# A second Strassen level for P2 beside P3 in the SwiGLU groups, with sums in dead tiles and an earlier state update in retention

## The chip, the cores and the metric

The kernel runs on one core of a Trainium2 chip. The metric is the device time of one execution in microseconds (us): before the change 2171.48 us is the median of three runs (2169.85 to 2172.43). The core has a matrix engine (TensorE, PE in the profile; PEld is its weight load), a vector engine (VectorE, DVE), a scalar engine (ScalarE, ACT), GpSimd (POOL), and SyncE (SP), which here issues the DMAs. Each engine takes its own instructions in the order in which the program lists them and waits on semaphores for what the others must deliver.

## The reference

One layer of a streaming encoder on x of 1024 tokens by 1024 channels, all in float32: a SwiGLU with weight 0.5, a mixing sub-layer, a second SwiGLU, a final norm.

```python
def swiglu_ffn(x, w_in, w_out):                      # D_FF = 2816
    gate, up = jnp.split(x @ w_in, 2, axis=-1)
    return (jax.nn.silu(gate) * up) @ w_out

h = h + 0.5 * swiglu_ffn(rmsnorm(h, norm_ffn1), ffn1_w_in, ffn1_w_out)
u = rmsnorm(h, norm_mix)
proj = u @ w_in                                      # q, k, v, g, p, two gates
ret = retention(q, k, v)                             # 4 heads, chunks of 64, decaying state
ret = head_norm(ret) * jax.nn.silu(g_ret)
pool_out = multiscale_pool(p, pool_w, pool_scale)    # windows 2, 4, 8, 16
merged = gate0 * (ret @ w_ret_up) + gate1 * (pool_out @ w_pool_up)
h = h + merged @ w_out
h = h + 0.5 * swiglu_ffn(rmsnorm(h, norm_ffn2), ffn2_w_in, ffn2_w_out)
return rmsnorm(h, norm_final)
```

In retention a state is carried over the tokens: `new_state = state * decay + k^T v`, and each chunk of tokens adds the product of its queries with the state before it.

## The kernel before

**Precision.** Every operand of a matmul is held as two tiles, a high half (a cast by ScalarE, line 151) and a low half (the source less that cast, by VectorE, line 152); `split` makes both. `mm3` (lines 171 to 173) issues three matmuls for one product: high by high, high by low, low by high. One product of a group is four `mm3`, that is 12 matmuls of 128x512.

**Strassen's scheme.** A group is a block of the weights, 1024 channels by two blocks of 128 columns, against all 1024 tokens. `strassen` computes it in Winograd's form with seven products in place of eight. The group's two weight blocks are loaded as raw tiles `ra` (L11, L12) and `rb` (L21, L22); the activations stand ready as R11, T2, T1, T3, R21, R22 and T4 (class `Next`). The group is a list of seven steps, each with a part that prepares weights and a part with the products: 0 P1 = L11 R11, 1 P6 = S2 T2, 2 P5 = S1 T1, 3 P7 = S3 T3, 4 P2 = L12 R21, 5 P3 = S4 R22, 6 P4 = L22 T4. Their sums form in PSUM banks a, b and e:

```python
S1 = L21 + L22;  S2 = S1 - L11;  S3 = L11 - L21;  S4 = L12 - S2
a = P1 + P2;  b = P1 + P6 (+ P5) + P3;  e = P7 + P4
BY_OPERAND = (0, 4, 1, 3, 2, 6, 5);  BY_SUM = (0, 3, 1, 4, 2, 6, 5)
```

**Pairs and the second level.** `pairs` (line 548) runs groups two by two. The first groups go step by step side by side (BY_OPERAND); from the group `start` on, P3 of both groups of a pair is left out of the single groups and done together by `third` (line 491): as both have the same operand R22, the two S4 stand side by side as one 2x2 block matrix, and seven products of quarter size (42 matmuls of 128x256) take the place of twice 12 of 128x512. The second level wants sums of the weights (`s12`, `s34`, lines 495 to 507, 128x256 pieces on VectorE) and differences of the blocks of R22, called y1 to y4. These four tiles are made once per operand by `Next.blocks` (line 329).

**The SwiGLUs.** In the first, the names begin with a: `ffn_in` "a" runs a plain group 0 and then groups 11, 1, 12, 2, 13, ... (21 of them), with start=4; in the second, they begin with c: 22 groups 0, 11, 1, 12, ..., start=2. A group's results are scaled by the norm's root (`rms`, line 639), gate goes through silu, and gate by up is the hidden block. When groups k and k + 11 are both there, the four differences that the down projection (`ffn_out`, "b" and "d") wants are made (lines 660 to 670) and stored to memory: t, b, r and m.

**What sets the order.** `Flow.run` takes the steps one by one: it calls the preparing part of a step four steps (LOOK) ahead of its products, and after each step's products up to two entries of a queue `flow.back`, in which scaling, silu, gating, the y blocks and the norm's work are put by `flow.add`. `flow.until` drains that queue until something named is ready. Evacuations of a bank are put in with high priority (`soon`), which sets them ahead in their engine's order. Tiles come from pools of a fixed number: 5 of weights, 4 raw, 9 of `t4` and 4 of `tl` (a thousand columns each), 8 of `c2` (512 columns), 6 + 2 PSUM banks. All loads and stores go out on SP's queue in program order.

**Retention.** For each of 4 heads there are two halves of the tokens (`Unit`, nh 0 and 1). `products` (line 1381) computes the first state (`update(0)`), the inner products, the part across chunks from that state (`across`, bank xb), and for nh 0 then the second state (`update(1)`). `update` (line 1357) runs 12 matmuls of 128x256 into a bank, copies or adds it to `now`, and splits that into high and low halves named `state`.

The functions that the change touches:

Of the kernel before, what the change touches and what calls it, by code (L numbers as in the profile page):

```python
# [89 lines left out]
def block_kernel(ctx: ExitStack, tc, x, x_tok, vecs, f1_in, f1_out, w_in, w_v, pool_w, w_ret, w_pool, w_o,  # L90
# [160 lines left out]
    class Next(Norm):  # L251


        def __init__(self, name, gain, keep=None):
            super().__init__(name)
            self.gain, self.keep = gain, keep
            self.M, self.Y, self.made, self.tiles, self.t1s, self.rb = {}, {}, {}, {}, {}, None

# [69 lines left out]

        def blocks(self):


            def differences(z):
                x = []
                for i in range(2):
                    m = self.M["R22", 2 * i + z]
                    x.append(c2(f"{self.name}x{i}{z}"))
                    tt(x[i], m[:, 0].bitcast(F32), m[:, 1].bitcast(F32), ADD)
                (x00, x01), (x10, x11) = ([half_of(v, j) for j in range(2)] for v in x)
                for n, p, q in (("y1", x01, x00), ("y3", x11, x01), ("y2", x11, None), ("y4", x10, None)):
                    if n not in self.made:  # L340

                        self.made[n] = sb.tile([P, 2, H], F32R, tag="tl", bufs=N_TL, name=f"{self.name}{n}")

                    to = {"y1": x00, "y3": x01, "y2": x00, "y4": x00}[n]
                    tt(to, p, x00 if q is None else q, SUB)
                    m, at = self.made[n], (LO, HI)[z]
                    split(m[:, 0, at], m[:, 1, at], to)
                if z:
                    self.Y.update(self.made)

            return [lambda z=z: differences(z) for z in range(2)]

        def block(self, n, z):

            if n in self.Y or isinstance(n, str):
                flow.until(lambda: n in self.Y)
                return parts(self.Y[n], (LO, HI)[z])
            return parts(self.operand("R22", 2 * n[0] + z), (LO, HI)[n[1]])

# [30 lines left out]

    def strassen(nx, wa, wb, name, evac, end, begin=None, shared=False):

# [14 lines left out]
        def prep_w(n):  # L407
            def go():
                if n == "L11":
                    blocks()  # L410
                elif n == "S2":
                    combine("S1", "L21", "L22", ADD)
                    combine("S2", "S1", "L11", SUB)
                elif n == "S3":
                    combine("S3", "L11", "L21", SUB)
                if n == "S4" or shared and n == "L22":
                    combine("S4", "L12", "S2", SUB)
                t["w", n] = weights(t[n], f"{name}w{n}")

            return go  # L420
# [56 lines left out]
        def last(f):  # L477
            def go():
                f()
                t["ends"] = t.get("ends", 0) + 1  # L480
                if t["ends"] == 2:
# [5 lines left out]
                   (prep_w("L12"), b2), (prep_w("S4"), last(b3)), (prep_w("L22"), last(b4))])  # L487
        g.t, g.name, g.third = t, name, last(lambda: evac((0, 1), t["b"], t.get("z")))
        return g

    def third(nx, A, B):

        w, t, a, b = {}, {}, A.t, B.t

        def prep1():
            w["x"] = weights(a["S4"], f"{A.name}wx")
            s = t["s"] = c2(f"{A.name}s12")
            tt(s[:, LO], b["S4"][:, LO], b["S4"][:, HI], ADD)
            tt(s[:, HI], s[:, LO], a["S4"][:, LO], SUB)
            w["s12"] = weights(s, f"{A.name}ws12")  # L500

        def prep2():
            s = c2(f"{A.name}s34")
            tt(s[:, LO], a["S4"][:, LO], b["S4"][:, LO], SUB)
            tt(s[:, HI], a["S4"][:, HI], t["s"][:, HI], SUB)
            w["s34"] = weights(s, f"{A.name}ws34")

        def prep3():
            w["y"] = weights(b["S4"][:, HI], f"{A.name}wy")

        def prod(dst, n, at, m, start=False):
            for z in range(2):
                mm3(dst, parts(w[n], at + z), nx.block(m, z), start and z == 0, z == 1)


        def one():
            x, y = (bank(f"{A.name}{n}") for n in "xy")
            t["x"] = x
            a["z"], b["z"] = c2(f"{A.name}z"), c2(f"{B.name}z")
            prod(x[:, LO], "x", 0, (0, 0), True)  # L520
            with soon():
                copy(a["z"][:, LO], x[:, LO])
            prod(y[:, HI], "s12", 0, "y1", True)
            with soon():
                copy(b["z"][:, HI], y[:, HI])
            prod(a["b"][:, LO], "x", 2, (1, 0))

        def two():
            x = t["x"]
            prod(x[:, LO], "s12", 2, "y2")  # L530
            with soon():
                tt(a["z"][:, HI], x[:, LO], b["z"][:, HI], ADD)
            prod(a["b"][:, HI], "s34", 2, (1, 1))
            with soon():
                A.third()

        def three():
            x = t["x"]
            prod(b["b"][:, LO], "y", 0, "y4")
            prod(x[:, LO], "s34", 0, "y3")  # L540
            with soon():
                copy(b["z"][:, LO], x[:, LO])
                tt(b["z"][:, HI], x[:, LO], b["z"][:, HI], ADD)
                B.third()

        return [(prep1, one), (prep2, two), (prep3, three)]


    BY_SUM = (0, 3, 1, 4, 2, 6, 5)

    def pairs(nx, groups, first, behind=2, start=2):


        groups = list(groups)
        for n in range(0, len(groups), 2):
            shared = start <= n < len(groups) - behind
            two = [g(shared) for g in groups[n : n + 2]]
            if n == 0:
                for m in first:
                    yield from (g[m] for g in two)  # L560
            if n == start - 2:
                flow.add(*nx.blocks())
            if n == 0:
                continue
            for g in two:
                yield from (g[m] for m in BY_SUM if m != 5 or not shared)
            if shared:
                yield from third(nx, *two)

# [48 lines left out]
    def ffn_in(nx, w, ops, name, start=None):  # L618
# [4 lines left out]
        def group(g):  # L623
            gate_up = []

            def evac(which, in0, in1):
                if not gate_up:
                    new = tl if start and g == 0 else t4
                    gate_up.extend((new(f"{name}g{g}"), new(f"{name}u{g}")))
                tile, j = which  # L630
                dst = half(gate_up[tile], j)
                if in1 is not None:
# [8 lines left out]
            def end():  # L641
                gate, up = gate_up

# [32 lines left out]
            if start and g == 0:  # L676
                return plain_group(nx, start, f"{name}{g}_", evac, end)
            return lambda shared: strassen(nx, w[g, 0], w[g, 1], f"{name}{g}_", evac, end, shared=shared)
# [297 lines left out]
    def project(kind, n):  # L976
# [5 lines left out]

        def evac(which, in0, in1):
            if not pair:
                pair.extend((t4(f"{name}A"), t4(f"{name}B")))
            tile, j = which
            dst = half(pair[tile], j)
            if in1 is not None:
# [85 lines left out]

        return lambda shared: strassen(mix, w_in[at], w_in[at + 1], name, evac, end, shared=shared)

# [114 lines left out]
    def projections():  # L1191
# [5 lines left out]
        for o in light[10:]:  # L1197
            g = project(*o)(False)
            yield from (g[m] for m in BY_SUM)
# [78 lines left out]
    class Unit:  # L1278
# [76 lines left out]
        def update(self, s):  # L1355

            b = bank(f"st{self.name}{s}")
            for i in range(2):
                for j in range(2):
                    o = j * HD + i * P  # L1360
                    mm3(b[:, i * HD : (i + 1) * HD], parts(self.kd[s], slice(o, o + P)), self.v(2 * s + j),
                        i == 0 and j == 0, j == 1)
            now = c2(f"sf{self.name}{s}")
            with soon():
# [4 lines left out]
                m = sb.tile([P, 2, H], F32R, tag="t4", bufs=N_T4, name=f"state{self.name}{s}")  # L1369
                split(m[:, 0], m[:, 1], now)  # L1370
            self.total = now
# [378 lines left out]
```

## Time and profile before

| what | value |
|---|---|
| median of three runs | 2171.48 us (2169.85 to 2172.43) |
| profiled execution, its own time | 2169.78 us |
| its span | 2168.0 us |
| granted TensorE clock, mean | 0.999 |
| TensorE busy | 2154.2 us, 99% |
| VectorE busy | 1797.7 us, 83% |
| ScalarE busy | 1041.7 us, 48% |
| instructions of TensorE, VectorE, ScalarE | 10510, 3098, 1908 |
| DMA, mean rate | 148 GB/s |

The profile is one execution as the hardware profiler took it. A row of the timeline reads: start, duration, engine, line, operation, output<-inputs, partitions by elements, and in brackets how long the engine had been idle before it and what released it. Ends of matmuls are modelled, so the distance between starts is the measure of what a matmul takes. VectorE's instructions too overlap a little in the records, so the same is done for them. In the names, a_ and c_ are the groups of the first and second SwiGLU with the group's number left out (wS: weights of a sum, wL: of a block, wx, ws, wy: of the second level), au, ag, cu, cg the up and gate tiles, n1, n2, n3 the operands of the first SwiGLU, the projections and the second SwiGLU. A row of waits reads: who waited for whom, total us, how many times, the longest.

### The profile page before, as it was taken

To read this page: it belongs to the slowest core of one execution; us is meant where nothing else is said; L and a number is where in the kernel's file an instruction comes from. 1 tells how busy PE (TensorE), PEld (TensorE's weight loads), DVE (VectorE), ACT (ScalarE), POOL (GpSimd) and SP (SyncE) were. 2 spreads that over 40 slices of the span, in tenths; PEclk is the share of its full clock that TensorE was granted. 3 is DMA by queue.
4 is the path that set the end of the run, shared out by engine and by line. 5 is a ranking of instruction groups with operands and counts; after the bars stand their busy time and mean duration, and the time that the engine had idled before them with its cause. 6 is when DMAs were issued, how large, how long until landed. Compare 5 with 4: busy or idle time off the path is not lost.

```text
span 2168.0 us, 29018 instructions
## 1 busy us (share of the span) xinstructions
PE 2154.2 (99%) x10510; PEld 1817.4 (84%) x10510; DVE 1797.7 (83%) x3098; ACT 1041.7 (48%) x1908; POOL 0.2 (0%) x4
## 2 busy tenths in 40 slices
PE   9999999999999999999999999999999999999998
PEld 7888888888888888888888888878888888888888
DVE  8797878888788797889768876799997878798774
ACT  8443434445555434434426763456644434344461
POOL 0000000000000000000000000000000000000000
PEclk9999999999999999999999999999999999999999
DMA  6233322596323233333585657524232322359522
GB/s 230 84 124 116 123 96 97 180 336 217 107 92 117 97 127 108 127 107 117 164 263 194 192 191 279 189 88 151 73 136 83 127 93 102 117 190 342 172 83 78
DMA packets 118256, 320.35 MB, mean 148 GB/s; under 512 B 13024, under 2 KB 18272, under 8 KB 118112
## 3 DMA queue, kind: packets, MB, share of 16 engines
q1 hardware_dynamic: 118112, 318.50, 42.9%
q8 instruction: 82, 1.34, 0.2%
q14 instruction: 62, 0.51, 0.1%
HBM read 227.75 MB, written 90.70 MB: 147 GB/s over the span
## 4 chain that ended last, share of the span: by engine, by line
PE 93%; DVE 4%; ACT 1%; DMA 1%; issue 1%; SPq 0%; DVEq 0%; ACTq 0%
PE c_b L171 2%; PE c_b L173 2%; PE c_b L172 2%; PE a_b L172 2%; PE a_b L171 2%; PE a_b L173 2%; PE c_e L171 2%; PE c_a L172 2%; PE c_a L171 2%; PE c_a L173 2%; PE c_e L173 2%; PE c_e L172 2%; PE a_a L172 2%; PE a_a L171 2%; PE a_e L172 2%; PE a_e L171 2%
## 5 line engine op out<-in xcount | busy, mean ns | idle before, releaser
L151 ACT CAST c_wS<-c_S 128x512 fp32r<-128x512 f32 x70 | 43.5, 622 | 73.8 <-DVE c_S L405 58.0
L172 PE MATMUL c_a<-n3R,c_wL 128*128 128x512 f32 x176 | 68.7, 390 | 0.0
L173 PE MATMUL c_a<-n3R,c_wL 128*128 128x512 f32 x176 | 68.5, 389 | 0.0
L172 PE MATMUL c_b<-n3T,c_wS 128*128 128x512 f32 x176 | 68.5, 389 | 0.0
L173 PE MATMUL c_b<-n3T,c_wS 128*128 128x512 f32 x176 | 68.5, 389 | 0.0
L171 PE MATMUL c_a<-n3R,c_wL 128*128 128x512 f32 x176 | 68.4, 390 | 0.0
L171 PE MATMUL c_b<-n3T,c_wS 128*128 128x512 f32 x176 | 68.1, 389 | 0.0
L151 ACT CAST a_wS<-a_S 128x512 fp32r<-128x512 f32 x68 | 42.1, 620 | 52.3 <-DVE a_S L405 30.3
L171 PE MATMUL a_a<-n1R,a_wL 128*128 128x512 f32 x168 | 65.5, 390 | 0.0
L172 PE MATMUL a_a<-n1R,a_wL 128*128 128x512 f32 x168 | 65.5, 390 | 0.0
L173 PE MATMUL a_a<-n1R,a_wL 128*128 128x512 f32 x168 | 65.4, 389 | 0.0
L171 PE MATMUL a_b<-n1T,a_wS 128*128 128x512 f32 x168 | 65.4, 389 | 0.0
L172 PE MATMUL a_b<-n1T,a_wS 128*128 128x512 f32 x168 | 65.4, 389 | 0.0
L173 PE MATMUL a_b<-n1T,a_wS 128*128 128x512 f32 x168 | 65.4, 389 | 0.0
L152 DVE TENSOR_TENSOR a_wS<-a_S,a_wS 128x512 fp32r<-128x512 f32 x68 | 46.4, 684 | 4.9 <-ACT a_wS L151 4.8
L152 DVE TENSOR_TENSOR c_wS<-c_S,c_wS 128x512 fp32r<-128x512 f32 x70 | 47.9, 684 | 1.1 <-ACT c_wS L151 1.0
L151 ACT CAST c_wL<-c_ra 128x512 fp32r<-128x512 f32 x44 | 27.2, 620 | 26.8 <-PE c_e L173 22.6
L151 ACT CAST a_wL<-a_ra 128x512 fp32r<-128x512 f32 x42 | 26.0, 621 | 27.2 <-PE a_e L173 22.4
L173 PEld LDWEIGHTS c_a<-n3R,c_wL 128*128 128x128 f32 x176 | 33.0, 188 | 6.9
L173 PEld LDWEIGHTS c_b<-n3T,c_wS 128*128 128x128 f32 x176 | 33.0, 188 | 6.9
L172 PEld LDWEIGHTS c_a<-n3R,c_wL 128*128 128x128 f32 x176 | 33.1, 188 | 6.8 <-DVE n3R L156 0.3
L172 PEld LDWEIGHTS c_b<-n3T,c_wS 128*128 128x128 f32 x176 | 33.0, 188 | 6.9
(2872 smaller groups left out, 7715.8 us busy)
## 6 DMA issues: line engine op xcount, KB each, us to landing
c_ra<-in_f_in SPq DMA_DIRECT2D x22, 512.0 KB, 3.6
c_rb<-in_f_in SPq DMA_DIRECT2D x22, 512.0 KB, 4.3
a_ra<-in_f_in SPq DMA_DIRECT2D x21, 512.0 KB, 3.9
a_rb<-in_f_in SPq DMA_DIRECT2D x21, 512.0 KB, 4.7
t<-au SPq DMA_DIRECT2D x11, 512.0 KB, 2.6
b<-an SPq DMA_DIRECT2D x11, 512.0 KB, 2.8
r<-au SPq DMA_DIRECT2D x11, 512.0 KB, 3.0
bra<-in_f_out SPq DMA_DIRECT2D x11, 512.0 KB, 5.9
```

Source lines behind the costliest of these rows:

```text
L151: copy(hi, src)
L152: tt(lo, src, hi.bitcast(F32), SUB)
L171: mm(dst, w[0], m[0], start=start, stop=False, skip_group_check=True)
L172: mm(dst, w[0], m[1], start=False, stop=False, skip_group_check=True)
L173: mm(dst, w[1], m[0], start=False, stop=stop, skip_group_check=True)
```

## The change

1. `third` becomes `common(nx, A, B, n)`, which does the second level for n = 3 (P3, S4 by R22, into bank b) and for n = 2 (P2, L12 by R21, into bank a).
2. `Next.blocks` takes the operand's name. With `over`, y1 is written over the second half of the columns of the operand's own first two tiles, which no product reads any more. Of the other three, those of R22 go to two `t4` tiles and a `tl` tile, those of R21 to three `tl` tiles.
3. `ffn_in` uses `pairs_of_both` in place of `pairs`: the first two groups run side by side as before (with an odd third group alone in the first SwiGLU), then the blocks of R22 are queued. The next pair, called alone, shares P3 only, and after its second P2 the blocks of R21 are queued. All further pairs run step 0 of both groups, the shared P2, steps 3, 1, 2 of one and then of the other group, the shared P3, and step 6 of both. P2 is so shared in 8 pairs of the first SwiGLU and 9 of the second, P3 in one pair more of each than before.
4. Sums go to tiles that nobody reads any more: S3 over L21, S4 over S2, s34 over S4. S1 is made ahead of whichever of S2 and S3 comes first; this holds for the projections and the merge too. The partial results of the second level go into the gate or up tile itself (`dest`), and the difference `n` of the hidden blocks goes into the gate tile.
5. In retention, for nh 0 the second state's update goes ahead of the inner products, and the first state is split from the PSUM bank itself.

```diff
-        def blocks(self):
+        def blocks(self, R, tags, over=False):
...
+                left = list(tags)
                 for n, p, q in (("y1", x01, x00), ("y3", x11, x01), ("y2", x11, None), ("y4", x10, None)):
...
+                    if n == "y1" and over:
+                        m, at = self.M[R, z], HI
+                    else:
+                        tag, bufs = left.pop(0)
...
                     split(m[:, 0, at], m[:, 1, at], to)
@@ strassen, prep_w
                 if n == "L11":
                     blocks()
-                elif n == "S2":
+                elif n in ("S2", "S3") and "S1" not in t:
                     combine("S1", "L21", "L22", ADD)
+                if n == "S2":
                     combine("S2", "S1", "L11", SUB)
                 elif n == "S3":
-                    combine("S3", "L11", "L21", SUB)
-                if n == "S4" or shared and n == "L22":
-                    combine("S4", "L12", "S2", SUB)
+                    t["S3"] = t["L21"]
+                    tt(t["S3"], t["L11"], t["L21"], SUB)
+                if n == "S4" or 3 in shared and n == "S1":
+                    t["S4"] = t["S2"]
+                    tt(t["S4"], t["L12"], t["S2"], SUB)
                 t["w", n] = weights(t[n], f"{name}w{n}")
...
-    def third(nx, A, B):
+    def common(nx, A, B, n):
+        src, to, which, R = ("L12", "a", (0, 0), "R21") if n == 2 else ("S4", "b", (0, 1), "R22")
         w, t, a, b = {}, {}, A.t, B.t
         def prep1():
-            w["x"] = weights(a["S4"], f"{A.name}wx")
+            w["x"] = weights(a[src], f"{A.name}wx{n}")
...
+            s = a[src] if n == 3 else c2(f"{A.name}s34{n}")
...
+            t["x"], t["A"], t["B"] = x, A.dest(which), B.dest(which)
             prod(x[:, LO], "x", 0, (0, 0), True)
             with soon():
-                copy(a["z"][:, LO], x[:, LO])
+                copy(t["A"][:, LO], x[:, LO])
...
-            prod(a["b"][:, LO], "x", 2, (1, 0))
+            prod(a[to][:, LO], "x", 2, (1, 0))
...
+    def pairs_of_both(nx, groups, first):
+        groups = list(groups)
+        A, B = (g(()) for g in groups[:2])
+        steps = [g[m] for m in first for g in (A, B)]
+        n = 2
+        if len(groups) % 2:
+            C = groups[n](())
+            steps += [C[m] for m in BY_SUM]
+            n += 1
+        tl_, t4_ = ("tl", N_TL), ("t4", N_T4)
+        steps[-1] = then(steps[-1], nx.blocks("R22", [t4_, tl_, t4_], True))
+        yield from steps
+        alone = True
+        for n in range(n, len(groups), 2):
+            A, B = (g((3,) if alone else (2, 3)) for g in groups[n : n + 2])
+            yield A[0]
+            yield B[0]
+            if alone:
+                yield A[4]
+                yield then(B[4], nx.blocks("R21", [tl_] * 3, True))
+            else:
+                yield from common(nx, A, B, 2)
+            for g in (A, B):
+                yield from (g[m] for m in (3, 1, 2))
+            yield from common(nx, A, B, 3)
+            yield A[6]
+            yield B[6]
+            alone = False
@@ ffn_in
-                    e["n"], e["m"] = t4(f"{name}n{k}"), c2(f"{name}m{k}")
+                    e["n"], e["m"] = gate, c2(f"{name}m{k}")
...
-            return chain(group(0), pairs(nx, (group(g) for g in order[1:]), BY_OPERAND, start=4))
-        return pairs(nx, (group(g) for g in order), BY_OPERAND)
+            return chain(group(0), pairs_of_both(nx, (group(g) for g in order[1:]), BY_OPERAND))
+        return pairs_of_both(nx, (group(g) for g in order), BY_OPERAND)
@@ Unit.update and products
                 if self.nh == 0 and s == 0:
+                    split(m[:, 0], m[:, 1], b)
                     copy(now, b)
                 else:
                     stt(now, self.total, float(np.exp(SPAN * LOG_DECAY[self.h])), b, MUL, ADD)
-                split(m[:, 0], m[:, 1], now)
+                    split(m[:, 0], m[:, 1], now)
...
             if self.nh == 1:
                 self.across(0, self.state)
+            else:
+                self.state = self.update(1)
             self.inner()
             self.across(1, mid)
-            if self.nh == 0:
-                self.state = self.update(1)
```

(`then(step, work)` is the step with the work put into the queue behind its products.)

More of the change, by code (lines that the diff above doesn't have):

```diff
@@ L256, in __init__ @@
             self.gain, self.keep = gain, keep
-            self.M, self.Y, self.made, self.tiles, self.t1s, self.rb = {}, {}, {}, {}, {}, None
+            self.M, self.Y, self.made, self.ready, self.tiles, self.t1s, self.rb = {}, {}, {}, set(), {}, {}, None
         def quarter(self, mt, tokens, tile):
@@ L508, in prep3, with prod @@
         def prep3():
-            w["y"] = weights(b["S4"][:, HI], f"{A.name}wy")
-        def prod(dst, n, at, m, start=False):
+            w["y"] = weights(b[src][:, HI], f"{A.name}wy{n}")
+        def prod(dst, k, at, m, start=False):
             for z in range(2):
-                mm3(dst, parts(w[n], at + z), nx.block(m, z), start and z == 0, z == 1)
+                mm3(dst, parts(w[k], at + z), nx.block(R, m, z), start and z == 0, z == 1)
         def one():
-            x, y = (bank(f"{A.name}{n}") for n in "xy")
-            t["x"] = x
-            a["z"], b["z"] = c2(f"{A.name}z"), c2(f"{B.name}z")
+            x, y = (bank(f"{A.name}{k}{n}") for k in "xy")
+            t["x"], t["A"], t["B"] = x, A.dest(which), B.dest(which)
@@ L555, in pairs @@
         for n in range(0, len(groups), 2):
-            shared = start <= n < len(groups) - behind
+            shared = (3,) if start <= n < len(groups) - behind else ()
             two = [g(shared) for g in groups[n : n + 2]]
@@ L561, in pairs @@
             if n == start - 2:
-                flow.add(*nx.blocks())
+                flow.add(*nx.blocks("R22", [("tl", N_TL)] * 4))
             if n == 0:
@@ L567, in pairs, with then, body @@
             if shared:
-                yield from third(nx, *two)
+                yield from common(nx, *two, 3)
+    def then(step, work):
+        def body():
+            step[1]()
+            flow.add(*work)
+        return step[0], body
+    def pairs_of_both(nx, groups, first):
[26 more added lines that the diff above has]
+            alone = False
     def two_by_two(groups, order, between=None):
@@ L623, in group, with dest @@
         def group(g):
-            gate_up = []
-            def evac(which, in0, in1):
[L627 to L631, printed above, removed]
+            gate_up = {}
+            def dest(which):
+                tile, j = which
+                if tile not in gate_up:
+                    gate_up[tile] = (tl if start and g == 0 else t4)(f"{name}{'gu'[tile]}{g}")
+                return half(gate_up[tile], j)
+            def evac(which, in0, in1):
+                j, dst = which[1], dest(which)
                 if in1 is not None:
@@ L981, in project, with dest, evac @@
         scaled = kind in "gpt"
-        def evac(which, in0, in1):
+        def dest(which):
             if not pair:
                 pair.extend((t4(f"{name}A"), t4(f"{name}B")))
-            tile, j = which
-            dst = half(pair[tile], j)
+            return half(pair[which[0]], which[1])
+        def evac(which, in0, in1):
+            j, dst = which[1], dest(which)
             if in1 is not None:
```

67 lines of the change are left out of this document (34 added, 33 removed).

## The prediction

> **What bounds the kernel now.** I read the page's busy time first, then the 40 slices, then the chain that ended last, then TensorE's waits.
>
> ```profile
> span 2168.0 us, 29018 instructions
> PE 2154.2 (99%) x10510; PEld 1817.4 (84%) x10510; DVE 1797.7 (83%) x3098; ACT 1041.7 (48%) x1908; POOL 0.2 (0%) x4
> ...
> PE   9999999999999999999999999999999999999998
> ...
> DVE  8797878888788797889768876799997878798774
> ...
> PE 93%; DVE 4%; ACT 1%; DMA 1%; issue 1%; SPq 0%; DVEq 0%; ACTq 0%
> ```
> ```profile
> PE xb L172 <- DVE state L152: 2.2, 3, 0.9
> PE wo1b L171 <- ACT wo1wS L151: 1.6, 1, 1.6
> ...
> PE wo1b L173 <- DVE wo1wS L152: 0.4, 1, 0.4
> ```
>
> TensorE is busy in every slice, and its largest waits in the whole span are 2.2 us in retention and 2.0 us at the first group of the output projection. So the time is TensorE's own work, and a microsecond of matmuls removed is worth a microsecond. VectorE is second with 83%; its slices reach 9 where a stage starts. The profiled run took 2169.8 us, 1.7 us under the median of the runs shown; the sum below starts from the former.
>
> **The gain in matmuls.** Starts of matmuls give the spacing (the second number of a row is a modelled duration and overlaps).
>
> ```profile
> 1720.94 0.39 PE L171 MATMUL c_e<-n3T,c_wS 128*128 128x512 f32 x1
> ...
> 1723.66 0.39 PE L171 MATMUL c_b<-n3T,c_wS 128*128 128x512 f32 x1
> ...
> 1901.66 0.28 PE L171 MATMUL c_x<-n3R,c_wx 128*128 128x256 f32 x1
> ...
> 1906.70 0.40 PE L171 MATMUL c_a<-n3R,c_wL 128*128 128x512 f32 x1
> ```
>
> The first two rows enclose one product of 12 matmuls of 512 columns: 2.72/12 = 0.2267 us each. The last two enclose a whole second level, 42 matmuls of 256 columns: 5.04/42 = 0.120 us each. One more use of the second level replaces 24 x 0.2267 = 5.44 us by 5.04 us and saves 0.40 us. In the order of the changed program TensorE has 456 fewer matmuls of 512 and 798 more of 256, that is 19 uses: P2 in 8 pairs of the first SwiGLU and 9 of the second, P3 in one more pair of each. 103.4 - 95.8 = **-7.6 us**. That is all there is to win from the idea.
>
> [...]
>
> **The price on VectorE.** Its spacing, again from starts:
>
> ```profile
> 1854.47 0.69 DVE L152 TENSOR_TENSOR c_wx<-c_S,c_wx 128x512 fp32r<-128x512 f32 x1 [1.29 <-ACT c_wx L151]
> ...
> 1882.39 0.69 DVE L405 TENSOR_TENSOR c_S<-c_S,c_ra 128x512 f32<-128x512 f32 x1
> ...
> 1887.20 0.68 DVE L639 TENSOR_TENSOR cu<-cu,n3rb 128x512 f32<-128x512 f32 x1
> ...
> 1892.17 0.69 DVE L152 TENSOR_TENSOR c_wx<-c_S,c_wx 128x512 fp32r<-128x512 f32 x1 [1.29 <-ACT c_wx L151]
> ```
> ```profile
> 1575.20 0.75 DVE L345 TENSOR_TENSOR n3x<-n3x,n3x 128x256 f32<-128x256 f32 x2
> 1575.87 0.68 DVE L405 TENSOR_TENSOR c_S<-c_ra,c_S 128x512 f32<-128x512 f32 x1
> ```
>
> Eight instructions of 512 columns start between 1882.39 and 1887.20: 4.81/8 = 0.602 us each. Two of 256 take 0.67: 0.335 each. The changed order has 65 more of 512 and 165 more of 256: 39.1 + 55.3 = 94.4 us more for VectorE. Whether it costs anything is decided by stage.
>
> *Steady pairs.* The two c_wx rows lie one pair apart: 37.70 us. Now VectorE has 45 x 0.602 + 7 x 0.335 = 29.4 us of work in it, then 48 x 0.602 + 14 x 0.335 = 33.6 us, against 120 x 0.2267 + 84 x 0.120 = 37.3 us of TensorE. So it fits, at 90%. The tightest point is S3 of the pair's second group. Both groups now load their four raw tiles at the start of the pair and there are four such buffers, so the chain is: L22 of the previous pair's first group is split, its raw tile comes free, SP loads the next pair's second L11 into it, ACT casts it, and 38 VectorE instructions later S3 is ready.
>
> ```profile
> c_ra<-in_f_in SPq DMA_DIRECT2D x22, 512.0 KB, 3.6
> ...
> a_ra<-in_f_in SPq DMA_DIRECT2D x21, 512.0 KB, 3.9
> ...
> bra<-in_f_out SPq DMA_DIRECT2D x11, 512.0 KB, 5.9
> ```
>
> With a landing of 3.6 to 3.9 us I walk this chain through with about 0.3 us to spare; with 4.5 us it would be 0.6 us late in each of 17 pairs, 10 us. Bounds 0 to 10; taken **+0.5**, near the end of the landings that the rows show.
>
> *Where a stage starts.* Here VectorE is full already:
>
> ```profile
> 80.00:120.00 40.00, 40.00 (x174) 32.41 (x173) 37.73 (x66) 19.13 (x30) 0.00 (x0) 1.00 0.25 80
> 120.00:160.00 40.00, 40.00 (x198) 33.98 (x197) 38.63 (x71) 18.63 (x35) 0.00 (x0) 1.00 0.35 132
> ```
> ```profile
> 1520.00:1560.00 40.00, 40.00 (x184) 32.84 (x183) 38.53 (x70) 23.35 (x44) 0.00 (x0) 1.00 0.27 90
> 1560.00:1600.00 40.00, 40.00 (x174) 32.17 (x173) 39.00 (x78) 18.55 (x34) 0.00 (x0) 1.00 0.27 99
> ```
> (Columns: window, its length, then busy time and instructions of TensorE, weight loads, VectorE, ScalarE and GpSimd, the clock, the DMA share, GB/s.)
>
> VectorE has 1.0 to 2.3 us free in 40. The change puts here the difference blocks of R21 beside those of R22 (per operand 4 instructions of 512 and 16 of 256: 2.41 + 5.36 = 7.8 us) and the second set of sums, of the first pair that shares P2 (4.2 us), behind the gating work that the first groups leave. Both engines take their work in order, so I count in the built program between two fixed points: an evacuation on VectorE that waits for the last matmul of a product, and a later matmul that waits for a VectorE result.
>
> First SwiGLU: from the evacuation of group 13's last product to the low half of group 14's S3 weights stand 40 instructions of 512 and 29 of 256 on VectorE, 24.1 + 9.7 = 33.8 us. TensorE has 62 matmuls of 512 and 58 of 256 in between, 14.1 + 7.0 = 21.0 us. It must wait **+12.8 us**; handing over adds some 0.3, an idle VectorE at the start could only add.
>
> Second SwiGLU: from the evacuation of group 11's bank e to that of group 12's bank b, behind which the next banks are taken, there are 51 of 512 and 38 of 256, 30.7 + 12.7 = 43.4 us. TensorE has 146 of 512 and 32 of 256, 36.9 us, and two matmuls that spread the norm's root:
>
> ```profile
> 1560.31 1.11 PE L230 MATMUL n30b<-n30dg,cst 128*128 128x512 f32 x2
> ...
> 1561.49 0.40 PE L173 MATMUL c_b<-n3R,c_wS 128*128 128x512 f32 x1
> ```
>
> One spread and one plain matmul fill 1.18 us here, so a spread takes 0.95, and TensorE has 38.8 us. The difference is 4.6, with the handoffs **+5**. By the same count the kernel before has no such deficit above 0.8 us except at the output projection, 2.5, where the trace shows 2.0. The bounds for both stages together: no gain can lie here, as TensorE is busy 40.00 of 40.00 in the windows above, so 0 below; above, all the added work uncovered, 2 x (7.8 + 4.2) = 24. I take the 17.8 of the count, because its two ends are fixed by order and its durations are rows.
>
> **The small edits.** *Retention.* The second state's update moves ahead of the inner products: 12 matmuls of 256 (1.4 us), one VectorE update and one split, no DMA, so SP's and GpSimd's queues are passed by nothing. These matmuls now cover the split of the first state for which the xb row waits, and the first state is split straight from the bank. Bounds 0 to -2.2; taken **-2.2**, as 1.4 us exceeds the longest single wait, 0.9. *S1, S4, S3 in other order* in the projections and the output projection: 0 to -2.0 by the wo1b rows; **-1**, since one of its two sums is gone ahead of S3. *Sums in dead tiles*: S3 over L21, S4 over S2, the parts of P2 and P3 in the gate and up tiles. No instruction is added; a raw tile is held until S3's weights are split, which is in the chain above. The stores of the hidden differences leave from the gate tile, equal in number and bytes. Nothing. *End of a stage.* The first loads for the down projection go out some 10 us later than now, behind the last pair's raw tiles, and land in 5.9 us:
>
> ```profile
> 440.00:480.00 40.00, 40.00 (x178) 33.10 (x178) 33.74 (x56) 16.68 (x31) 0.00 (x0) 1.00 0.97 349
> ```
>
> With the DMA at 97% there, 0 to 4; **+1**, as four steps of matmuls still lie ahead of their use.
>
> **Sum.** 2169.8 - 7.6 - 2.2 - 1.0 + 12.8 + 5.0 + 1.0 + 0.5 = 2178.3 on the profiled run's scale, 2180.0 on the median's; I say **2179**.
>
> **The rivals.**
> 1. *Faster: the starts are absorbed.* If VectorE drains its backlog ahead of the two fixed points (the blocks fall into idle time of earlier steps), both waits fall to 3 us together and the median is 2171.5 - 9.3 + 3 = 2165 (9.3: the other terms of the sum). For it: the work is only 8 us per operand, and the 90% of steady pairs leaves room. Against it: the count above starts at an instruction that cannot run earlier. It decides below 4.9 us of waits in the two starts. Chance 0.10.
> 2. *Half of it.* The starts cost 5 to 13.6 us, because some of VectorE's work is not behind the fixed points: 2167 to 2176, within 0.2% (4.3 us, about what a measurement of this kernel can tell from no change). Chance 0.18.
> 3. *Slower still: S3 late in each pair.* Landings of 4.5 us or more, as both groups' loads now go out together: 17 x 0.6 = 10 us, 2189. Against it: the second SwiGLU's DMA share is 0.25 to 0.37 in the windows above. Chance 0.12.
> 4. *A slow clock behind the long waits.* At the very start, after idling, 12 matmuls of 512 take 4.30 us, 0.358 each:
>
> ```profile
> 1.21 4.30 PE L193 MATMUL set<-zero 128*128 128x512 bf16 x12 [1.21 <-DVE zero L188]
> ```
>
> If a wait of several microseconds brings this pace back, each costs 12 x 0.13 = 1.6 us more, with three such waits 5: 2184. [...] Chance 0.15.
>
> The forecast itself, 2176 to 2183, has 0.45. Cases 3 and 4 and the forecast end slower: 0.72; within 0.2%: 0.18; faster: 0.10. The range, 2168 to 2191, takes in case 2 from below and case 3 from above and leaves out case 1 and two mishaps at once.
>
> **What would show it.** In the changed profile, matmuls of 256 still 0.120 apart, and a steady pair's period of 37.3 us; TensorE below 38 of 40 in one or two windows near 90 to 160 and near 1560 to 1620, waiting for VectorE's splits of a_wS, x or y tiles, with VectorE at 39 or more; no xb row above 0.5. I am wrong if VectorE has idle time inside those windows while TensorE does not wait, if TensorE waits for a_wS or c_wS in every pair, or if the 256-column matmuls come slower than 0.120 among mixed banks.

## The result, and the profile after

The changed kernel takes 2206.95 us, the median of six runs (2204.98 to 2209.92), against 2170.66 us before: a ratio of 1.0166, 95% interval 1.0155 to 1.0177. It is slower by 36 us. The forecast was slower by 8, with a range up to 2191 us; the way was right, the size was not, and the time lies outside the range. The profiled execution took 2209.92 us, the longest of the six, with a span of 2208.1 us, 40.1 us more than the 2168.0 us before.

The page of the changed kernel, first the span and the busy times, then TensorE and VectorE by slices, then the chain:

```profile
span 2208.1 us, 30086 instructions
...
PE 2167.5 (98%) x10852; PEld 1832.1 (83%) x10852; DVE 1888.7 (86%) x3328; ACT 1081.9 (49%) x2019; POOL 0.2 (0%) x4
...
PE   9989999999999999999999999999989999999998
...
DVE  8798989999779798899767886899998989999874
...
PE 90%; DVE 6%; ACT 2%; DMA 1%; issue 1%; SPq 0%; DVEq 0%; ACTq 0%
```

VectorE has 91 us more to do, close to the 94.4 of the sum, and TensorE now has two more slices under 90%, near the start of either SwiGLU. Its waits:

```profile
PE c_b L171 <- ACT c_v L455: 12.0, 10, 5.9
PE a_b L171 <- ACT a_v L455: 5.4, 8, 0.7
PE a_a L173 <- DVE a_wL L152: 5.2, 1, 5.2
PE a_e L171 <- ACT a_wS L151: 2.2, 1, 2.2
```

Two kinds are seen here: a few long waits, and one short wait that comes again and again on the same tile, the copy v. The windows (length, then busy time and instructions of TensorE, weight loads, VectorE, ScalarE and GpSimd, then clock, DMA share, GB/s) show where each lies:

```profile
120.00:160.00 40.00, 30.37 (x138) 24.04 (x137) 38.82 (x83) 17.41 (x38) 0.00 (x0) 0.87 0.22 82
...
200.00:240.00 40.00, 39.33 (x211) 33.67 (x210) 35.75 (x65) 17.64 (x33) 0.00 (x0) 1.00 0.29 99
...
1600.00:1640.00 40.00, 33.53 (x154) 27.75 (x153) 36.52 (x79) 18.48 (x39) 0.00 (x0) 0.91 0.20 65
...
1720.00:1760.00 40.00, 39.32 (x218) 34.03 (x218) 35.50 (x65) 18.01 (x34) 0.00 (x0) 1.00 0.30 100
```

In two windows, one at the start of either SwiGLU, TensorE is idle for 9.6 and 6.5 us and its clock falls to 0.87 and 0.91. In nearly every later window of these halves 0.67 us are missing, about one short wait for each pair.

By stage (from the first matmul of a stage to the first of the next, at the end to the last matmul) the time went as follows. "Matmuls" is the number of matmuls by their undisturbed spacing; "lost" is what the starts are apart beyond it.

| stage | before, us | after, us | difference | matmuls | lost |
|---|---|---|---|---|---|
| first SwiGLU, up | 398.57 | 421.43 | +22.9 | 397.6 to 394.0 | 1.0 to 27.4 |
| first SwiGLU, down | 209.44 | 209.44 | 0.0 | | |
| projections and values | 533.28 | 533.35 | +0.1 | | |
| retention | 198.90 | 197.52 | -1.4 | | |
| merge, output projection | 155.45 | 155.61 | +0.2 | | |
| second SwiGLU, up | 419.87 | 437.87 | +18.0 | 417.2 to 413.2 | 2.7 to 24.7 |
| second SwiGLU, down | 216.52 | 216.52 | 0.0 | | |

The matmuls got cheaper by 3.6 + 4.0 = 7.6 us, just what the sum has. Everything that went wrong is loss in the two upward halves, about 48.5 us more. Split at the first of the recurring waits (157.8 and 1652.4 us), 24.4 us of it lie at the starts and 24.1 us in the 17 steady pairs.

**The recurring wait.** TensorE around one of them (the timeline of the changed kernel: start, duration, engine, line, operation):

```profile
1691.04 0.39 PE L172 MATMUL c_b<-n3T,c_wS 128*128 128x512 f32 x1
1691.27 0.39 PE L173 MATMUL c_b<-n3T,c_wS 128*128 128x512 f32 x1
1692.33 0.50 PE L171 MATMUL c_b<-n3T,c_wS 128*128 128x512 f32 x1 [0.68 <-ACT c_v L455]
1692.67 0.39 PE L172 MATMUL c_b<-n3T,c_wS 128*128 128x512 f32 x1
```

And ScalarE at the same time:

```profile
1691.70 0.59 ACT L455 COPY c_v<-c_b 128x512 f32<-128x512 f32 x1 [2.13 <-PE c_b L173]
1692.78 0.62 ACT L151 CAST c_wS<-c_rb 128x512 fp32r<-128x512 f32 x1 [0.50 <-DVE c_rb L426]
```

P6 ends in bank b; ScalarE copies the bank to v; P5 adds to the same bank, and begins when the copy is done: the copy ends at 1692.29, P5 starts at 1692.33. ScalarE is free, idle for 2.13 us before, and starts 0.43 us after the start of P6's last matmul. The two starts are 1.06 us apart in place of 0.23, and the next spacing is 0.34: 0.83 + 0.11 = 0.95 us for each of 17 waits, 16.2 us. The second group of each pair has six matmuls of P3 between its P6 and P5 and loses 0.23, 3.9 us in all. Most of what is left of the 24.1 us, some 3 us, is lost at bank x of the shared P2, which VectorE reads between two products (line 547): the starts of the 256-column matmuls are up to 0.56 us apart there in place of 0.120. In the kernel before the list of steps was 0, 3, 1, 4, 2: P2, 12 matmuls on another bank, stood between. The change takes P2 out of that place, as it is now shared ahead of both groups, and runs 3, 1, 2.

**The long waits.** The timeline of TensorE at the start of the first and of the second SwiGLU:

```profile
129.66 0.28 PE L173 MATMUL a_b<-n1R22y,a_wy 128*128 128x256 f32 x1
135.12 0.79 PE L173 MATMUL a_a<-n1R,a_wL 128*128 128x512 f32 x1 [5.18 <-DVE a_wL L152]
135.71 0.63 PE L171 MATMUL a_a<-n1R,a_wL 128*128 128x512 f32 x1
136.14 0.63 PE L172 MATMUL a_a<-n1R,a_wL 128*128 128x512 f32 x1
...
150.29 0.50 PE L171 MATMUL a_e<-n1T,a_wS 128*128 128x512 f32 x1 [2.17 <-ACT a_wS L151]
...
1617.50 0.28 PE L173 MATMUL c_x<-n3R22y,c_ws 128*128 128x256 f32 x1
1623.67 0.80 PE L171 MATMUL c_b<-n3T,c_wS 128*128 128x512 f32 x1 [5.90 <-ACT c_v L455]
```

The first of them waits for the weights of a block; VectorE in that time works through the blocks of R22 and then of R21 (the low halves n1R22y and n1R21y) with evacuations between; the low half of the awaited weights stands behind them:

```profile
131.50 0.42 DVE L152 TENSOR_TENSOR n1R21y<-n1x,n1R21y 128x256 fp32r<-128x256 f32 x1
...
132.77 0.42 DVE L152 TENSOR_TENSOR n1R21y<-n1x,n1R21y 128x256 fp32r<-128x256 f32 x1
...
134.37 0.69 DVE L152 TENSOR_TENSOR a_wL<-a_ra,a_wL 128x512 fp32r<-128x512 f32 x1
```

The last looks like the recurring wait but is another: the copy v stands on ScalarE behind the casts of the blocks of R21, and these wait for VectorE's differences:

```profile
1621.02 0.40 ACT L151 CAST n3R<-n3x 128x256 fp32r<-128x256 f32 x1 [1.20 <-DVE n3x L345]
...
1621.90 1.21 ACT L151 CAST n3R21y<-n3x 128x256 fp32r<-128x256 f32 x3
1623.04 0.59 ACT L455 COPY c_v<-c_b 128x512 f32<-128x512 f32 x1
```

Behind the wait of 5.18 us the starts of the 512-column matmuls are 0.427 us apart in place of 0.227 until 140.8, behind the wait of 5.90 us until 1629.0, and again from 151.4 to 154.6. The granted clock reads 0.50 in 135 to 141, 151.4 to 154.6 and 1623.6 to 1629, and 1.00 in 141 to 150. Some 33 matmuls run at the slow pace and cost 6.8 us of the 24.4.

### The profile page after: what moved, and what is told of

It is laid out like the page before. It is cut to its first block, busy times and chain, and to the rows that moved or that the text cites. A ratio compares the mean times of both kernels' runs of the same rounds, so it can differ in the third digit from the quotient of the medians.

```text
span 2208.1 us, 30086 instructions
## 1 busy us (share of the span) xinstructions
PE 2167.5 (98%) x10852; PEld 1832.1 (83%) x10852; DVE 1888.7 (86%) x3328; ACT 1081.9 (49%) x2019; POOL 0.2 (0%) x4
## 4 chain that ended last, share of the span: by engine, by line
PE 90%; DVE 6%; ACT 2%; DMA 1%; issue 1%; SPq 0%; DVEq 0%; ACTq 0%
PE c_b L171 2%; PE c_b L173 2%; PE c_b L172 2%; PE a_b L171 2%; PE a_b L173 2%; PE a_b L172 2%; PE c_e L171 2%; PE c_e L172 2%; PE c_e L173 2%; PE a_e L173 2%; PE a_e L172 2%; PE a_e L171 2%; PE dp6b L171 1%; PE dp6b L172 1%; PE dp6b L173 1%; PE bp6b L171 1%
## 5 line engine op out<-in xcount | busy, mean ns | idle before, releaser
L171 PE MATMUL c_b<-n3T,c_wS 128*128 128x512 f32 x176 | 71.5, 408 | 12.0 <-ACT c_v L455 12.0
L173 PE MATMUL c_b<-n3T,c_wS 128*128 128x512 f32 x176 | 69.7, 396 | 0.0
L172 PE MATMUL c_b<-n3T,c_wS 128*128 128x512 f32 x176 | 69.5, 395 | 0.0
L171 PEld LDWEIGHTS c_b<-n3T,c_wS 128*128 128x128 f32 x176 | 33.5, 191 | 24.1 <-ACT c_v L455 17.7
L173 PE MATMUL a_a<-n1R,a_wL 128*128 128x512 f32 x104 | 41.7, 403 | 5.2 <-DVE a_wL L152 5.2
L171 PEld LDWEIGHTS a_b<-n1T,a_wS 128*128 128x128 f32 x168 | 31.5, 187 | 16.4 <-ACT a_v L455 10.5
L171 PE MATMUL a_a<-n1R,a_wL 128*128 128x512 f32 x104 | 41.5, 399 | 0.0
L172 PE MATMUL a_a<-n1R,a_wL 128*128 128x512 f32 x104 | 41.4, 398 | 0.0
L172 PE MATMUL c_a<-n3R,c_wL 128*128 128x512 f32 x104 | 40.6, 390 | 0.0
L173 PE MATMUL c_a<-n3R,c_wL 128*128 128x512 f32 x104 | 40.5, 389 | 0.0
L171 PE MATMUL c_a<-n3R,c_wL 128*128 128x512 f32 x104 | 40.5, 389 | 0.0
L173 PEld LDWEIGHTS c_b<-n3T,c_wS 128*128 128x128 f32 x176 | 33.6, 191 | 7.4
L151 ACT CAST c_ws<-c_s 128x512 fp32r<-128x512 f32 x28 | 17.4, 623 | 45.4 <-DVE c_s L514 33.9
L172 PEld LDWEIGHTS c_b<-n3T,c_wS 128*128 128x128 f32 x176 | 33.7, 191 | 6.5
L173 PEld LDWEIGHTS a_b<-n1T,a_wS 128*128 128x128 f32 x168 | 31.5, 188 | 6.8
L172 PEld LDWEIGHTS a_b<-n1T,a_wS 128*128 128x128 f32 x168 | 31.6, 188 | 6.1
L171 PE MATMUL a_e<-n1T,a_wS 128*128 128x512 f32 x84 | 33.4, 397 | 2.2 <-ACT a_wS L151 2.2
L151 ACT CAST a_ws<-a_s 128x512 fp32r<-128x512 f32 x25 | 15.5, 624 | 40.2 <-DVE a_s L514 30.0
L152 DVE TENSOR_TENSOR a_wS<-a_S,a_wS 128x512 fp32r<-128x512 f32 x45 | 30.5, 692 | 5.4 <-ACT a_wS L151 5.4
```

Source lines behind the costliest of these rows:

```text
L151: copy(hi, src)
L152: tt(lo, src, hi.bitcast(F32), SUB)
L171: mm(dst, w[0], m[0], start=start, stop=False, skip_group_check=True)
L172: mm(dst, w[0], m[1], start=False, stop=False, skip_group_check=True)
L173: mm(dst, w[1], m[0], start=False, stop=stop, skip_group_check=True)
```

## The experiments

Two theories stand against each other for the steady pairs. A: P5 has lost the matmuls that stood between it and P6. B: VectorE, at 90%, sets the period, and the copy v is only where it shows. For the starts: A has VectorE's backlog from the blocks and the first sums; C says that this backlog is merely put off when the work is moved, since VectorE has no room.

**P7 between P6 and P5.**

```diff
             for g in (A, B):
-                yield from (g[m] for m in (3, 1, 2))
+                yield from (g[m] for m in (1, 3, 2))
```

> The changed kernel with one edit: in the further pairs and the pair alone the steps of a group run 1, 3, 2 (P6, P7, P5) in place of 3, 1, 2 (P7, P6, P5), so that the 12 matmuls of P7 (2.7 us) stand between P6 and P5 on the same bank b. Theory A (P5 may not add to bank b before ScalarE's copy v of it is done; the wait costs 0.95 us for the first group of each of 17 pairs and 0.23 for the second): the 0.68 us waits on c_v and a_v vanish, the pair's period falls from 38.7 to about 37.5 us, and the time to 2183 to 2191 us. Rival B (VectorE, at 90%, sets the pair's period and the copy is only where it shows): the wait moves to another tile, the period stays above 38.4, the time above 2201.

Measured: 2185.42 us (2183.56 to 2186.31), a ratio of 1.0068 to the kernel before, 1.0053 to 1.0083. The recurring waits are gone: TensorE's largest waits are now

```profile
PE a_a L173 <- DVE a_wL L152: 5.2, 1, 5.2
PE c_b L171 <- ACT c_v L455: 4.3, 1, 4.3
PE a_b L171 <- ACT a_wS L151: 2.4, 2, 2.2
```

and a steady window is full, with VectorE busier than in the changed kernel (36.60 against 35.75 us of 40):

```profile
200.00:240.00 40.00, 40.00 (x218) 34.82 (x217) 36.60 (x67) 19.54 (x36) 0.00 (x0) 1.00 0.31 99
```

The pair's period, from one shared P3 to the next, is 37.25 us, the matmuls' own 37.28; in the changed kernel it is 38.7 and before 37.70. So theory A holds, VectorE does not set the period, and the steady pairs do gain the 0.4 us that the idea promised. The long waits stay.

**P3 alone.** The second level of P2 is left out, the rest of the change kept:

```diff
             if alone:
                 yield A[4]
-                yield then(B[4], nx.blocks("R21", [tl_] * 3, True))
+                yield B[4]
...
-            alone = False
```

> The changed kernel without the second level of P2: every pair after the first groups is run as the pair alone (P3 shared, P2 twice 12 matmuls of 512), and no blocks of R21 are made. The order of steps, the sums in dead tiles and retention stay as changed. Theory A (the steady loss is P5 behind P6 on one bank, the loss at the starts is VectorE's backlog from the blocks of R21 and the first sums of P2): the 17 waits on the copy v stay at 0.68 us, the waits of 5 us near 130 and 1620 vanish, and the 6.8 us of matmuls come back: 2206 - 20 + 7 = about 2193. Rival B (P2's second level loads VectorE in every pair): the periods lose all waits and the time falls to 2174 to 2180.

Measured: 2175.45 us (2174.6 to 2176.89), ratio 1.0022, 1.0013 to 1.0032. The long waits vanished as theory A had it, but so did the 17 short ones, which A had wrong, and the time is that of B. The order of the built programs says why. It is made at the build by a planner that estimates when things are ready, and it puts other matmuls in front of one that would wait, if their operands are ready. The matmuls between P6 and P5 of the first and of the second group of a steady pair:

```
kernel                        first group     second group
before                        12 of 512       12 of 512
changed                        0               6 of 256
P7 between                    12 of 512       12 of 512
P3 alone                       4 of 512        6 of 256
```

With P3 alone the planner slips four matmuls of the second group's P7 (into bank e) in, 0.91 us, and that is enough but for 0.05 us in the next spacing:

```profile
1738.96 0.39 PE L173 MATMUL c_b<-n3T,c_wS 128*128 128x512 f32 x1
1739.18 0.39 PE L171 MATMUL c_e<-n3T,c_wS 128*128 128x512 f32 x1
...
1740.09 0.44 PE L171 MATMUL c_b<-n3T,c_wS 128*128 128x512 f32 x1
```

The second groups keep their 0.23 us, so the pair's period is 37.96 us, still above the 37.70 of the kernel before; a start wait of 1.7 us with slow matmuls behind it adds to that.

In the changed kernel the planner had none to put there: the rows above show the second group's S3 weights (c_wS from c_rb) being cast at 1692.78, after P6 had ended. So the wait has two conditions: the list puts P5 straight behind P6, and S3 of the second group is ready too late to be put between. Four settings agree on the price: no matmul between, 0.95 us; 0.72 us of matmuls, 0.23; 0.91 us, 0.05; 2.72 us, nothing. The trace of the changed kernel also shows what this S3 waits for. The load of its raw tile goes out at 1668.57, and such loads landed within 4.9 us there; VectorE makes S3 only at 1692.01, after 20 us without a pause:

```profile
1668.57 0.33 SPq L134 DMA_DIRECT2D c_rb<-in_f_in  x1
...
1692.01 0.70 DVE L426 TENSOR_TENSOR c_rb<-c_ra,c_rb 128x512 f32<-128x512 f32 x1
...
1672.00:1692.00 20.00, 19.57 (x105) 16.54 (x104) 20.00 (x37) 8.45 (x16) 0.00 (x0) 1.00 0.29 103
```

It is so in every pair that shares P2 but the first of either SwiGLU. So S3 stands behind VectorE's other work and not behind a load. Which part of that work puts it there, the sums of P2 above all, was not tried by itself.

**Two pairs alone.** P2 is shared one pair later:

```diff
-        alone = True
+        alone = 2
...
-                yield then(B[4], nx.blocks("R21", [tl_] * 3, True))
+                yield then(B[4], nx.blocks("R21", [tl_] * 3, True)) if alone == 1 else B[4]
...
-            alone = False
+            alone = max(alone - 1, 0)
```

> The changed kernel with two pairs alone in place of one: P2 is shared one pair later in each SwiGLU, and the blocks of R21 are queued behind the second P2 of the second such pair. All else as changed. Theory A: the two starts lose most of their 17 us of waits and the 7 us of slow clock behind them, at 0.8 us more of matmuls; the 0.68 us waits of the pairs stay: 2186 to 2192. Rival C (the backlog is only put off by a pair, since VectorE has no room in any pair): waits of 5 us appear about 38 us later, and the time stays at 2203 to 2208.

Measured: 2189.41 us (2189.04 to 2190.56), ratio 1.0090, 1.0073 to 1.0106: theory A again. The short waits are as they were; of the waits at the starts the longest left is one of 1.7 us:

```profile
PE c_b L171 <- ACT c_v L455: 5.7, 9, 0.7
PE a_b L171 <- ACT a_v L455: 5.3, 9, 0.7
PE a_e L171 <- ACT a_wS L151: 1.7, 1, 1.7
```

**Both edits.**

> The edits of the two kernels before this together: steps 1, 3, 2 and two pairs alone. If the two causes are separate, their gains add: 2164 to 2176, at or below the kernel before. If they share slack on VectorE (S2 is now wanted 2.7 us earlier in each pair), a part is given back: 2177 to 2186.

Measured: 2169.92 us (2168.09 to 2174.76), ratio 0.9997, 0.9988 to 1.0007: no difference to the kernel before. The gains of the two edits, 21.5 and 17.5 us, would give 2167.9 if they added in full; nearly all of it comes, so the two causes are separate. In the trace, whose execution took 2174.76 us and is the longest of the ten, 10.1 us are still lost in the first SwiGLU, with waits of 2.0 and 1.8 us at its start, and the slow pace behind one of them.

**No work for the blocks of R21.** In `Next.blocks` VectorE's sums, differences and low halves are left out for R21:

```diff
-                    x.append(c2(f"{self.name}x{i}{z}"))
-                    tt(x[i], m[:, 0].bitcast(F32), m[:, 1].bitcast(F32), ADD)
+                    x.append(c2(f"{self.name}x{i}{z}") if R == "R22" else m[:, 0])
+                    if R == "R22":
+                        tt(x[i], m[:, 0].bitcast(F32), m[:, 1].bitcast(F32), ADD)
...
-                    tt(to, p, x00 if q is None else q, SUB)
+                    if R == "R22":
+                        tt(to, p, x00 if q is None else q, SUB)
...
-                    split(m[:, 0, at], m[:, 1, at], to)
+                    if R == "R22":
+                        split(m[:, 0, at], m[:, 1, at], to)
+                    elif not (n == "y1" and over):
+                        src = self.M[R, z]
+                        copy(m[:, 0, at], src[:, 0, LO].bitcast(F32))
+                        copy(m[:, 1, at], src[:, 1, LO].bitcast(F32))
```

> The changed kernel, in which the blocks of R21 are not computed: their tiles are filled by 12 copies on ScalarE instead, and VectorE does nothing for them, so the shared P2 gives wrong values. All else, the order 3, 1, 2 with its waits too, is as changed. If the 7.8 us of VectorE's work for these blocks are what the starts wait for, the count in the built order leaves 5.5 to 6.4 us of deficit near 130 to 150 in place of 12.8 to 14.2 and none above 3 in the second SwiGLU: 2207 - 8 - 6 and less slow clock, 2187 to 2194. If the sums of P2 and the gating were the larger part, it stays above 2198.

Measured: 2191.38 us in one run. Both waits of over 5 us are gone, and the clock of both windows reads 1.00:

```profile
120.00:160.00 40.00, 36.14 (x181) 28.87 (x180) 38.17 (x76) 21.36 (x49) 0.00 (x0) 1.00 0.27 96
1600.00:1640.00 40.00, 39.33 (x214) 33.90 (x213) 39.37 (x77) 22.04 (x47) 0.00 (x0) 1.00 0.27 89
```

So the 7.8 us of VectorE's work for these blocks, in one piece, cost some 15.6 us over the two starts, slow pace included, by this one run against the median of six. What is left in the first window, waits of 1.1 and 0.9 us for S-weights, is put down to the blocks of R22 and the sums; that was not tried by itself, but the next kernel, which moves the blocks of R22, has no such wait there.

**A plain pair first.** Both edits, and in the first SwiGLU one more pair that shares nothing, with the blocks of R22 behind its P3:

```diff
...
+        r22 = nx.blocks("R22", [t4_, tl_, t4_], True)
+        plain = len(groups) % 2
+        if not plain:
+            steps[-1] = then(steps[-1], r22)
...
+            A, B = (g(() if plain else (3,) if alone else (2, 3)) for g in groups[n : n + 2])
...
+            if plain:
+                yield A[5]
+                yield then(B[5], r22)
+            else:
+                yield from common(nx, A, B, 3)
```

> Steps 1, 3, 2 and two pairs alone, as in the kernel of both edits, and in the first SwiGLU one more pair, run ahead of those two, shares nothing: the blocks of R22 are queued only behind its two whole P3. In the built order VectorE then has no deficit above 0.5 us against TensorE in the first SwiGLU (the kernel of both edits: 4 to 6 us near its start). Theory A (the starts lose by VectorE's backlog alone): of the 10.1 us that TensorE loses in the first SwiGLU of the kernel of both edits some 7 vanish with the slow clock behind them, against 0.8 us of matmuls: 2161 to 2166, under the kernel before by 5 to 10. Rival C (the backlog comes back at the first pair that shares P2): a wait of 2 us or more there, 2167 to 2171.

Measured: 2164.23 us (2163.85 to 2165.69), ratio 0.9973, 0.9962 to 0.9984: faster than both kernels, by 6 us than the one before. Only 3.1 us are lost in the first SwiGLU of its trace:

```profile
120.00:160.00 40.00, 40.00 (x197) 33.81 (x196) 33.87 (x65) 18.08 (x35) 0.00 (x0) 1.00 0.29 99
160.00:200.00 40.00, 40.00 (x197) 33.84 (x196) 39.94 (x77) 17.55 (x34) 0.00 (x0) 1.00 0.30 104
```

VectorE is just as full in the second window, at 39.94 of 40, but TensorE has no wait there: the same work, the blocks of R22 one pair later and those of R21 two pairs later than in the change, is hidden. So the backlog does not come back a pair later, as C had it.

**Retention's edit alone**, put into the kernel before as it stands in the change.

> The kernel before with retention's edit alone (the second state's update ahead of the inner products, the first state split from the bank). The sum took 2.2 us for it: about 2168.9 against 2171.1, retention's stage 2.2 us shorter than 198.9. The profile of the changed kernel has this stage 1.4 us shorter; if that is the edit's whole worth, 2169.7.

Measured: 2170.11 us (2167.7 to 2170.71), ratio 0.9997, 0.9987 to 1.0006, too little for the measurement. In the trace the stage is 197.49 us in place of 198.90, as in the changed kernel. The xb waits fell from 2.2 to 0.5 us, and two others came:

```profile
PE ot L1423 <- ACT o L1401: 1.0, 1, 1.0
...
PE s L171 <- ACT o L1401: 0.5, 2, 0.3
...
PE xb L172 <- DVE state L152: 0.5, 1, 0.5
```

In the kernel before, the second update stood between `across` and the transposes (ot); with it moved ahead, the transposes and the next scores (s) wait for ScalarE's work on the outputs.

## Why the prediction was right or wrong

- *Bound by TensorE, 19 uses, 0.40 us each, -7.6 us*: right. The matmuls' part of the two stages fell by 3.6 and 4.0 us, and with the waits gone the pair's period is 37.25 us against 37.28 in the sum.
- *Steady pairs +0.5 us, bounds 0 to 10*: wrong; this step failed. It measured +24.1. The step walked VectorE's chain to S3 and found 0.3 us to spare, and VectorE indeed does not set the pair's period. But it looked at VectorE alone. It did not ask what TensorE's own order had hidden: P2 is not only 24 matmuls that become cheaper, it is also what stood between P6 and P5 on one bank. The list of the changed steps, 3, 1, 2, says it, and the built order shows not one matmul between. The trace of the kernel before would have given an estimate: a copy v starts 0.42 us after the start of P6's last matmul (1704.78 to 1705.20) and takes 0.59, and a matmul starts 0.06 after the end of a cast that it waits for (9.80 to 9.86), with 0.33 in place of 0.227 to the next start. Less the one spacing of 0.227 that is some 0.9 us a pair, 15 us or more in 17 pairs. With it the sum would have been some 2194, still 13 us under what was measured. The bounds did not hold it because they were drawn around another mechanism. On the profiled run's scale the forecast was 2178.3 and the measurement 2209.9, 31.6 more: 23.6 from this step, 6.8 from the slow pace, and the rest from the small terms below.
- *Starts +12.8 and +5 us*: right in cause and, for the waits, in size: 24.4 us lost less 6.8 us of slow pace are 17.6, against 17.8. By start it is 11.1 and 6.5, where 12.8 and 5 were forecast, so that the sum fits this well is in part luck: one error makes up for the other. The place in the second SwiGLU was a little off, as the wait fell on the copy v behind ScalarE's casts rather than on the weights of s34.
- *The slow clock, a rival of its own with 5 us*: it came, with 6.8 us, behind the waits of 5.18 and 5.90 us and also behind one of 2.17. The rival had it as an alternative; with waits of 5 us forecast, its price belonged in the sum. That such waits bring the pace was a guess at the time: in the trace of the kernel before no wait after the start is longer than 1.6 us. Its price was of another make: 12 matmuls of 0.13 us behind each of three waits, from a row of bf16 matmuls; measured were some 33 matmuls of 0.20.
- *Retention -2.2*: -1.4, as two new waits on ScalarE's outputs take the rest. *Merge and output projection -1*: +0.2; the output projection gained 1.05 us, and the merge lost 1.2 by a wait of the same kind; with the same code for the merge, the traces of P7 between and of P3 alone have no such loss, so it hangs on the timing and is no fixed price of the edit. *End of a stage +1*: 0, both downward halves are unchanged within 0.01 us.
- *Rival 3, S3 late in each pair*: the second group's S3 was late, but no matmul waited for it. It was late for the planner, which so had nothing to put before P5. The rival's reason, slow landings, did not come (c_rb landed in 4.0 us and a_rb in 4.5 in the median, against 4.3 and 4.7 before): S3 waited for VectorE's queue. The prediction read this reason too kindly in any case. It went by the landings of ra, 3.6 and 3.9 us, while S3 needs rb as well, which landed in 4.3 and 4.7 us in the same list; and its windows show a DMA share of 0.27 for the second SwiGLU, not 0.25 to 0.37.

## What to carry to other kernels

When a product is taken out of its place to be made cheaper, ask what it was hiding: here 12 matmuls were the cover of a copy between two accumulations in the same bank, and a gain of 0.40 us a pair met a wait of 0.95. Count in the built order, for every bank that is read in the middle of its accumulation, how much work stands between the last matmul ahead of the read and the first behind it. And spread a block of one-off work for the second engine over several steps: the 7.8 us for R21's blocks cost some 15 us over the two starts right behind those of R22, and next to nothing when they came a pair or two later.

## What the runs showed of the hardware

- A bank that ScalarE copies between two matmuls into it costs TensorE 0.95 us where nothing stands between: 0.83 us of gap and 0.11 us in the next spacing. 0.91 us of other matmuls hide it but for 0.05, 0.72 us leave 0.23.
- After a wait of 5.2 or 5.9 us matmuls of 512 columns run 0.427 us apart in place of 0.227, for 5 to 6 us in the changed kernel; with P7 between, the pace lasted 3 to 4 us behind waits of 5.2 and 4.3 us. Waits of about 2 us brought the same pace in some kernels (behind 2.02 us with both edits, 1.74 us followed by 0.24 with P3 alone, 1.74 us followed by 0.38 with two pairs alone, and 2.17 us followed by 0.42 in the changed kernel) and did not in others (2.17 and 0.42 us with P7 between, 1.75 and 0.36 us with both edits), so by these runs the length of a wait of about 2 us does not tell whether the pace comes.
